# Attention of layer 2: the high and low parts of the values in one stationary operand, their products summed at the eviction

## The chip, the cores and the metric

The kernel runs on one core of a Trainium2 chip. The metric is device time in microseconds (us) of one execution. A core has five engines with a queue each, which work through it in order and meet at semaphores: PE (TensorE, matrix products), DVE (VectorE), ACT (ScalarE), POOL (GpSimd) and SP (SyncE, which here only issues DMAs). PE writes its products to PSUM, and ACT and DVE carry them from there to SBUF. Below, to evict means to read a result out of PSUM and write it to SBUF.

## The reference, cut to what matters

One inference step of two layers: a retention layer, then a layer of sliding-window attention, each for a prompt of 1024 tokens and for 8 decoding sequences of one token. The change is in the attention of the prompt in the second layer. There are 16 query heads of 64 elements and two key/value heads; eight query heads share one key/value head. A block of 128 queries sees its own block of keys and the one before it:

```python
scores = einsum('bnqkgd,bnskd->bnkgqs', qb, kk) * 64 ** -0.5      # 128 queries x 256 keys
scores = scores - alibi_slopes * dist                             # outside the band: -1e30
p = sink_softmax(scores, sinks)
o = einsum('bnkgqs,bnskd->bnqkgd', p, vv)                         # the product that is changed
y = x + (o * silu(gate)) @ w_out
```

Everything is computed to float32 accuracy. PE's fast format keeps fewer bits, so the kernel splits an operand x into a high part h (x rounded to the fast format) and a low part l = x - h, and forms a product of two such operands as h·h + h·l + l·h. That makes three passes through PE for each product.

## The kernel before, in words

Layer 1 and its output projection take the first two thirds of the time. Layer 2 begins with the keys and values: `kv_mm` projects them for eight chunks of 128 tokens, and `kv_ev` (lines 1269 to 1281) splits the values of a chunk into `vvh` (ACT, line 1272) and `vvl` (DVE, line 1273).

Then the heads are taken in pairs, eight pairs in all, and each pair in eight chunks of 128 queries, c = 0 to 7; a pair and a chunk make a unit, so there are 64 units. A generator (`pair_proj`) projects q and the gate of the next pair in steps of one slice of the weights, and the loop at the end of the program weaves three parts of three different units between these steps. In iteration m it does:

- `att_s` of unit m+4: four matmuls for the scores of both heads (lines 1477 and 1478), the scores scaled and biased to the tile `s` by DVE (line 1480, one instruction for each head), the negated row maximum by DVE (`mx`, line 1482), the exponentials with their sums by ACT (line 1484, two), the reciprocal of the sums by DVE (line 1485), and the division by POOL (line 1486);
- `att_x` of unit m+1: four transposes on PE (line 103 out to `tr`), their high part `pth` by ACT (line 1500) and low part `ptl` by DVE (line 1501);
- `att_o` of unit m: the products with the values. For each of the two key blocks (one block where c is 0) PE does three matmuls into the PSUM tile `o` of 64 partitions and 256 columns, which are 128 queries of each of the two heads: `vvh`·`pth`, `vvl`·`pth`, `vvh`·`ptl` (lines 1516 to 1518). ACT evicts the two heads to the two halves of `ot` (line 1521, two instructions of 64 partitions by 128 columns, scaled by 0.5), and POOL multiplies with the gate (line 1522). The last chunk of each token group writes `ot` to DRAM, issued by ACT (line 1527).

Between these parts `fill` puts steps of the projection for about 0.95 us each. `o` has one PSUM bank, so the matmuls of a unit wait until the tile of the unit before it is evicted; `sc` and `tr` have two. The evictions of the projection stand on ACT (lines 1365 to 1367, 1410) and DVE (lines 1368, 1370, 1408, 1411). From unit 50 on the low parts of the last weights are made by DVE (line 1061) instead of POOL, and from unit 59 on the steps woven in are those of the output projection. Reloads of earlier pairs from DRAM (`reload3`, lines 1617 to 1619) and the attention of the decoding sequences (from line 1540) fall there too.

The order of PE's instructions is that of the program text (`manual_schedule` over PE alone). The order on ACT, DVE, POOL and SP is chosen by a scheduler when the program is built, and is fixed from then on: an instruction that waits holds up all that stand behind it on its engine.

## Time and profile before

| | |
|---|---|
| median of 3 runs | 1365.5 us (1363.65 to 1366.26) |
| the profiled execution | 1365.26 us, of which the span of instructions is 1363.5 us |
| PE busy | 1309.2 us, 96% of the span |
| weight loads (PEld) busy | 1247.8 us, 92% |
| DVE busy | 742.0 us, 54% |
| ACT busy | 670.0 us, 49% |
| POOL busy | 760.6 us, 56% |
| granted PE clock, mean | 0.991 of full speed |
| attention of layer 2 | from about 985 to 1276 us of the span |

The busy time of an engine is the union of its instructions. A row of the table of groups names the line of the program, the engine, the operation, out<-in, the shape, the number of instructions, then the busy time of all and the mean time of one; behind the bar stands the time the engine sat idle just before such instructions, and what ended it. A row "A <- B" of the table of waits says that instructions A began when B was done, with the total time, how often, and the longest. Matmuls are pipelined: one lasts longer in the records than the distance from its start to the start of the next, and this distance is what a matmul costs in a dense stretch. DVE and ACT overlap neighbours a little as well.

### The profile page before, as it was taken

What the parts mean: (1) busy time and instruction counts of PE and PEld (TensorE: products, weight loads), DVE (VectorE), ACT (ScalarE), POOL (GpSimd) and SP (SyncE); (2) the same over time, 40 slices, a digit from 0 to 9 for tenths busy, and PEclk for the clock granted to TensorE, in tenths of its full rate; (3) what the DMA queues carried; (4) which work ended last, traced back from release to release, by engine and by line L of the source; (5) the groups of instructions that cost most, each with busy time, mean ns of one, the idle gap of its engine ahead of it and who ended that gap; (6) DMA issues with size and microseconds to landing.
All of it is one profiled execution on the core that took longest, in us unless ns stands there. A gap on an engine that the chain in (4) does not pass through costs nothing.

```text
span 1363.5 us, 25993 instructions
## 1 busy us (share of the span) xinstructions
PE 1309.2 (96%) x9541; PEld 1247.8 (92%) x9541; DVE 742.0 (54%) x1434; ACT 670.0 (49%) x1690; POOL 760.6 (56%) x886
## 2 busy tenths in 40 slices
PE   6999999999999999897979999998999999999998
PEld 6999999999999999686867889997999999998998
DVE  6943665666566553675762112325567777779421
ACT  5532545555556653575750111244476666667311
POOL 6753656656565763597986464563366666544000
PEclk9999999999999999899999999999999999999999
DMA  6314767677676752565645444461111110112532
GB/s 219 103 55 145 218 208 230 173 225 232 188 232 187 233 166 84 184 175 186 171 154 170 124 147 126 132 187 48 51 47 47 44 47 32 49 33 90 173 83 82
DMA packets 192803, 186.66 MB, mean 137 GB/s; under 512 B 12724, under 2 KB 172524, under 8 KB 192660
## 3 DMA queue, kind: packets, MB, share of 16 engines
q1 hardware_dynamic: 155776, 147.82, 36.1%
q10 hardware_dynamic: 36900, 37.19, 8.6%
q8 instruction: 75, 1.23, 0.4%
q14 instruction: 52, 0.43, 0.1%
HBM read 128.59 MB, written 57.41 MB: 136 GB/s over the span
## 4 chain that ended last, share of the span: by engine, by line
PE 81%; DVE 6%; POOL 4%; DMA 4%; ACT 2%; issue 2%; SPq 0%; ACTq 0%; POOLq 0%; DVEq 0%
PE b L340 7%; PE b L342 7%; PE b L341 7%; PE pj L1071 5%; PE pj L1072 5%; PE pj L1073 5%; PE b L334 4%; PE b L333 4%; PE b L335 4%; PE pj L1122 4%; PE pj L1120 4%; PE pj L1121 4%; PE tr L103 3%; POOL wl L1061 1%; PE tr L862 1%
## 5 line engine op out<-in xcount | busy, mean ns | idle before, releaser
L340 PE MATMUL b<-xh,woh 128*128 128x258 f32 x784 | 222.2, 283 | 0.0
L342 PE MATMUL b<-xh,wol 128*128 128x258 f32 x784 | 221.7, 283 | 0.0
L341 PE MATMUL b<-xl,woh 128*128 128x258 f32 x784 | 221.4, 282 | 0.0
L1071 PE MATMUL pj<-A_hi,wh 128*128 128x384 f32 (+1 forms) x512 | 171.7, 335 | 1.9 <-ACT Qd L1375 1.9
L1072 PE MATMUL pj<-A_lo,wh 128*128 128x384 f32 (+1 forms) x512 | 164.8, 322 | 0.0
L1073 PE MATMUL pj<-A_hi,wl 128*128 128x384 f32 (+1 forms) x512 | 164.7, 322 | 0.0
L1061 POOL TENSOR_TENSOR wl<-wr,wh 128x512 fp32r<-128x512 f32 (+1 forms) x68 | 125.4, 1857 | 53.3 <-DVE wh L1060 22.3
L340 PEld LDWEIGHTS b<-xh,woh 128*128 128x128 f32 x784 | 148.1, 189 | 1.1
L341 PEld LDWEIGHTS b<-xl,woh 128*128 128x128 f32 x784 | 148.7, 190 | 0.0
L342 PEld LDWEIGHTS b<-xh,wol 128*128 128x128 f32 x784 | 148.0, 189 | 0.0
L334 PE MATMUL b<-wol,xh 128*128 128x256 f32 x448 | 126.0, 281 | 1.2 <-DVE wol L224 1.2
L333 PE MATMUL b<-woh,xh 128*128 128x256 f32 x448 | 125.8, 281 | 0.0
L335 PE MATMUL b<-woh,xl 128*128 128x256 f32 x448 | 125.7, 281 | 0.0
L1486 POOL TENSOR_TENSOR s<-s,sm 128x512 f32<-128x512 f32 x64 | 67.7, 1059 | 75.4 <-DVE sm L1485 71.5
L282 POOL TENSOR_TENSOR yl<-yd,yh 128x256 fp32r<-128x256 f32 x64 | 56.4, 882 | 83.8 <-PE od L289 39.0
L1071 PEld LDWEIGHTS pj<-A_hi,wh 128*128 128x128 f32 x512 | 97.0, 189 | 2.4 <-ACT Qd L1375 2.2
L1072 PEld LDWEIGHTS pj<-A_lo,wh 128*128 128x128 f32 x512 | 97.0, 189 | 0.0
L1073 PEld LDWEIGHTS pj<-A_hi,wl 128*128 128x128 f32 x512 | 96.8, 189 | 0.0
L224 POOL TENSOR_TENSOR wol<-raw,woh 128x512 fp32r<-128x512 f32 x52 | 68.8, 1330 | 48.1 <-ACT woh L219 48.0
L334 PEld LDWEIGHTS b<-wol,xh 128*128 128x128 f32 x448 | 84.3, 188 | 1.4 <-DVE wol L224 1.4
L333 PEld LDWEIGHTS b<-woh,xh 128*128 128x128 f32 x448 | 84.3, 188 | 0.7
L335 PEld LDWEIGHTS b<-woh,xl 128*128 128x128 f32 x448 | 84.4, 188 | 0.0
(366 smaller groups left out, 3826.3 us busy)
## 6 DMA issues: line engine op xcount, KB each, us to landing
raw<-in_w_in_ret_dram ACTq DMA_DIRECT2D x44, 512.0 KB
st<-in_state_ret_dram SPq DMA_DIRECT2D x64, 256.0 KB
out_dram<-st SPq DMA_DIRECT2D x64, 256.0 KB
wr<-in_w_out_ret_dram SPq DMA_DIRECT2D x32, 512.0 KB
wr<-in_w_in_swa_dram SPq DMA_DIRECT2D x18, 512.0 KB
vb<-vscr SPq DMA_DIRECT2D x64, 128.0 KB
evp<-qks SPq DMA_DIRECT2D x32, 256.0 KB
evx<-vsc SPq DMA_DIRECT2D x32, 256.0 KB
```

What stands on the lines that cost most here:

```text
L224: eng.tensor_tensor(lo, src_of(s, name, sub), hi.bitcast(F32), SUB)
L333: mm(dst, xh, wh, start=a and i == 0, stop=False, skip_group_check=True)
L334: mm(dst, xh, wl, start=False, stop=False, skip_group_check=True)
L335: mm(dst, xl, wh, start=False, stop=z, skip_group_check=True)
L340: mm(dst, wh, xh, start=a, stop=False, **sg)
L341: mm(dst, wh, xl, start=False, stop=False, **sg)
L342: mm(dst, wl, xh, start=False, stop=z, **sg)
L1061: lo_eng[0].tensor_tensor(lo[:, js, :], raw[:, i:i + step, :], hi.bitcast(F32)[:, js, :], ALU.subtract)
L1071: mm(ps, hi[:, k, fs], xh[:, k, t0:t1], start=first and k == ks[0], stop=False)
L1072: mm(ps, hi[:, k, fs], xl[:, k, t0:t1], start=False, stop=False)
L1073: mm(ps, lo[:, k, fs], xh[:, k, t0:t1], start=False, stop=last and k == ks[-1])
L1486: nc.gpsimd.tensor_tensor(st[:, :, 0:256], st[:, :, 0:256], sm.unsqueeze(2).broadcast_to([128, 2, 256]), ALU.mult)
```

## The change

The values of a chunk now lie in one tile `vv`, with the high and the low part of each key/value head side by side: 64 columns high, 64 columns low. One matmul with this operand of 128 columns gives `vvh`·`pth` in the partitions 0 to 63 of `o` and `vvl`·`pth` in the partitions 64 to 127. The pass with `ptl` goes to the partitions 0 to 63 as before. So `o` has 128 partitions, a key block needs two matmuls in place of three, and the two halves have to be added at the eviction. ACT copies the upper half of the two heads, scaled by 0.5, to SBUF (one head to a new tile `t0`, one to its place in `ot`), and DVE adds the lower half to each (`scalar_tensor_tensor`, 64 partitions by 128 columns, one operand in PSUM). The tile `t0` has one buffer.

```diff
-        nc.scalar.activation(vvh[:, c, :], ps[:, 128:256], AF.Copy, scale=r)
-        nc.vector.scalar_tensor_tensor(vvl[:, c, :], ps[:, 128:256], r, vvh.bitcast(F32)[:, c, :],
-                                       ALU.mult, ALU.subtract)
+        pv = ps[:, 128:256].rearrange("p (g d) -> p g d", g=2)
+        nc.scalar.activation(vv[:, c, :, 0, :], pv, AF.Copy, scale=r)
+        nc.vector.scalar_tensor_tensor(vv[:, c, :, 1, :], pv, r, vvf[:, c, :, 0, :], ALU.mult, ALU.subtract)
...
-        po = opp.tile([64, 256], F32, tag="o", name="o")
-        vs = slice(u.g * 64, u.g * 64 + 64)
-        for hf in hs:
-            kc = c - 1 + hf
+
+        po = opp.tile([128, 256], F32, tag="o", name="o")
+        def pv(hf, low, **kw):
+            vs = vv[:, c - 1 + hf, u.g]
             rs_ = slice(hf * 256, hf * 256 + 256)
-            mm(po, vvh[:, kc, vs], pth[:, rs_], start=(hf == hs[0]), stop=False)
-            mm(po, vvl[:, kc, vs], pth[:, rs_], start=False, stop=False)
-            mm(po, vvh[:, kc, vs], ptl[:, rs_], start=False, stop=(hf == 1))
+            if low:
+                mm(po[0:64], vs[:, 0, :], ptl[:, rs_], start=False, **kw)
+            else:
+                mm(po, vs.rearrange("p a d -> p (a d)"), pth[:, rs_], **kw)
+
+        if c > 0:
+            pv(0, False, start=True, stop=False)
+            pv(0, True, stop=False)
+            pv(1, True, stop=False)
+            pv(1, False, start=False, stop=True)
+        else:
+            pv(1, False, start=True, stop=True)
+            pv(1, True, stop=True, skip_group_check=True)
         cs = slice(i * 128, i * 128 + 128)
+        t0 = atp.tile([128, 128], F32, name="t0", bufs=1)
+        t = (t0[64:128], ot[64:128, cs])
         for j in range(2):
-            nc.scalar.activation(ot[j * 64:j * 64 + 64, cs], po[:, j * 128:j * 128 + 128], AF.Copy, scale=0.5)
+            nc.scalar.activation(t[j], po[0:64, j * 128:j * 128 + 128], AF.Copy, scale=0.5)
+        for j in range(2):
+            nc.vector.scalar_tensor_tensor(ot[j * 64:j * 64 + 64, cs], po[64:128, j * 128:j * 128 + 128], 0.5, t[j],
+                                           ALU.mult, ALU.add)
         nc.gpsimd.tensor_tensor(ot[:, cs], ot[:, cs], gt[:, cs], ALU.mult)
```

In the changed kernel the lines behind the first hunk are one higher, and those behind `att_o` 16 higher: the scores stand in line 1481, the maximum in 1483, the reciprocal in 1486, `ptl` in 1502, ACT's copies in 1534 and DVE's additions in 1536.

DVE, a unit without projection work behind its scores (chunk 5 of the third pair). Before, the scores of one unit (`s`, two heads), their maximum, the `ptl` of an earlier unit, the reciprocal of the sums (`sm`), and then the scores of the next unit:

```order
L1480 SCALAR_TENSOR_TENSOR s_13431<-sc_13430,rq_13105,ndp_12837 128x256
L1480 SCALAR_TENSOR_TENSOR s_13431<-sc_13430,rq_13105,ndp_13131 128x256
L1482 TENSOR_REDUCE mx_13432<-s_13431 128x2
L1501 TENSOR_TENSOR ptl_13458<-tr_13452,pth_13457 128x512
L1485 RECIPROCAL sm_13433<-sm_13433 128x2
L1480 SCALAR_TENSOR_TENSOR s_13492<-sc_13491,rq_13185,ndp_12837 128x256
```

The same place now:

```order
L1481 SCALAR_TENSOR_TENSOR s_13450<-sc_13449,rq_13117,ndp_12845 128x256
L1481 SCALAR_TENSOR_TENSOR s_13450<-sc_13449,rq_13117,ndp_13144 128x256
L1483 TENSOR_REDUCE mx_13451<-s_13450 128x2
L1502 TENSOR_TENSOR ptl_13477<-tr_13471,pth_13476 128x512
L1486 RECIPROCAL sm_13452<-sm_13452 128x2
L1536 SCALAR_TENSOR_TENSOR ot_13433<-o_13486,t0_13491 64x128
L1536 SCALAR_TENSOR_TENSOR ot_13433<-o_13486,ot_13433 64x128
L1481 SCALAR_TENSOR_TENSOR s_13512<-sc_13511,rq_13198,ndp_12845 128x256
```

The two additions stand between the reciprocal of one unit and the scores of the next.

DVE, the place where the output products of two units (chunks 6 and 7 of the second pair) follow each other closely on PE. Before, with `sq` and `gt` the gate of the projection:

```order
L1485 RECIPROCAL sm_13264<-sm_13264 128x2
L1408 TENSOR_TENSOR sq_13331<-pj_13254,rbc_11586 128x384
L1480 SCALAR_TENSOR_TENSOR s_13316<-sc_13315,rq_13105,ndp_12837 128x256
L1480 SCALAR_TENSOR_TENSOR s_13316<-sc_13315,rq_13105,ndp_13131 128x256
L1411 SCALAR_TENSOR_TENSOR gt_13333<-gt_13333,sq_13331 128x384
L1482 TENSOR_REDUCE mx_13317<-s_13316 128x2
L1501 TENSOR_TENSOR ptl_13340<-tr_13336,pth_13339 128x256
```

The same place now:

```order
L1486 RECIPROCAL sm_13279<-sm_13279 128x2
L1409 TENSOR_TENSOR sq_13347<-pj_13269,rbc_11585 128x384
L1536 SCALAR_TENSOR_TENSOR ot_13313<-o_13314,t0_13319 64x128
L1536 SCALAR_TENSOR_TENSOR ot_13313<-o_13314,ot_13313 64x128
L1481 SCALAR_TENSOR_TENSOR s_13332<-sc_13331,rq_13117,ndp_12845 128x256
L1481 SCALAR_TENSOR_TENSOR s_13332<-sc_13331,rq_13117,ndp_13144 128x256
L1412 SCALAR_TENSOR_TENSOR gt_13349<-gt_13349,sq_13347 128x384
L1483 TENSOR_REDUCE mx_13333<-s_13332 128x2
L1502 TENSOR_TENSOR ptl_13356<-tr_13352,pth_13355 128x256
L1536 SCALAR_TENSOR_TENSOR ot_13313<-o_13359,t0_13364 64x128
L1536 SCALAR_TENSOR_TENSOR ot_13313<-o_13359,ot_13313 64x128
```

The additions of chunk 6 stand behind `sq`, ahead of the scores; those of chunk 7 behind the `ptl` of that place.

PE, the products of chunk 6. Before:

```order
L1516 MATMUL o_13299<-pth_13234,vvh_11582 64x256
L1517 MATMUL o_13299<-pth_13234,vvl_11583 64x256
L1518 MATMUL o_13299<-ptl_13235,vvh_11582 64x256
L1516 MATMUL o_13299<-pth_13234,vvh_11582 64x256
L1517 MATMUL o_13299<-pth_13234,vvl_11583 64x256
L1518 MATMUL o_13299<-ptl_13235,vvh_11582 64x256
```

The same place now, with the first step of the projection behind it:

```order
L1520 MATMUL o_13314<-pth_13248,vv_11582 128x256
L1518 MATMUL o_13314<-ptl_13249,vv_11582 64x256 x2
L1520 MATMUL o_13314<-pth_13248,vv_11582 128x256
L1071 MATMUL pj_13269<-A_hi_7708,wh_12907 128x384
L1072 MATMUL pj_13269<-A_lo_7709,wh_12907 128x384
```

Six matmuls have become four; what stands before and behind them on PE is as it was.

More of the change, by code (lines that the diff above doesn't have):

```diff
@@ L1232, in _trunk @@
     kkl = kvp.tile([128, 2, NP], F32R, name="kkl")
-    vvh = kvp.tile([128, 8, 128], F32R, name="vvh")
-    vvl = kvp.tile([128, 8, 128], F32R, name="vvl")
+    vv = kvp.tile([128, 8, 2, 2, 64], F32R, name="vv")
+    vvf = vv.bitcast(F32)
     kdd = kvp.tile([8, 128], F32, name="kdd")
```

## The prediction

> **What bounds the kernel now.** I read the page first, then the busy time in windows, the waits of PE and DVE, the groups, the timeline of one pair, and the chain that ended last.

> ```profile
> span 1363.5 us, 25993 instructions
> PE 1309.2 (96%) x9541; PEld 1247.8 (92%) x9541; DVE 742.0 (54%) x1434; ACT 670.0 (49%) x1690; POOL 760.6 (56%) x886
> ```

> The averages make PE the bound and DVE half idle. The change lies in one stage only, so I took windows there (core 0: PE, PEld, DVE, ACT, POOL busy, then PE clock, DMA share, GB/s): the start of the attention, its even part, one pair of heads in it, and its end.

> ```profile
> 966.00:985.00 19.00, 17.14 (x104) 16.71 (x103) 11.10 (x23) 7.22 (x24) 5.29 (x7) 0.91 0.01 2
> 985.00:1222.00 237.00, 235.43 (x1714) 232.04 (x1713) 170.21 (x369) 160.82 (x476) 148.89 (x214) 1.00 0.13 41
> 1102.53:1139.34 36.81, 36.81 (x273) 36.42 (x271) 26.69 (x59) 22.95 (x71) 19.98 (x33) 1.00 0.09 29
> 1222.40:1262.40 40.00, 36.80 (x281) 35.11 (x281) 37.97 (x80) 29.33 (x83) 18.69 (x24) 1.00 0.29 90
> ```

> A pair takes 36.81 us, and PE is busy in all of it; the even part of 237 us is 237 / 36.81 = 6.44 such pairs. DVE is busy for 26.69 us of a pair, 73%. At the end, from 1222.4 to 1262.4, it is DVE that is full: 37.97 of 40 us. The chain that ended last says the same; in the even part it is matmuls, here it steps from DVE to DVE:

> ```profile
> 1255.02 0.59 DVE wl L1061
> 1255.61 1.15 DVE rbc L1564
> 1256.76 0.79 DVE s L1480 x2
> 1257.55 0.59 DVE ptl L1501
> 1258.14 1.13 DVE t L1568
> ```

> So there are two stages with two limits, and the change takes from PE and gives to DVE. What DVE waits for inside the pair (1102.53 to 1139.34), in total, times and longest:

> ```profile
> DVE s L1480 <- PE sc L1478: 4.0, 4, 1.9
> DVE sm L1485 <- ACT s L1484: 2.0, 5, 0.6
> DVE qs L1368 <- ACT qs L1367: 1.8, 3, 1.4
> DVE gt L1411 <- ACT gt L1410: 0.8, 2, 0.5
> DVE ptl L1501 <- ACT pth L1500: 0.6, 2, 0.3
> ```

> Of 10.12 idle us (36.81 - 26.69) only 4.0 are waits for the scores from PE. The others are waits for ACT, inside a queue that runs in order.

> **PE's part: 120 matmuls fewer.**

> ```profile
> L1516 PE MATMUL o<-pth,vvh 128*64 128x256 f32 x120 | 35.0, 292 | 3.1 <-ACT ot L1521 3.1
> L1517 PE MATMUL o<-pth,vvl 128*64 128x256 f32 x120 | 33.4, 278 | 0.0
> L1518 PE MATMUL o<-ptl,vvh 128*64 128x256 f32 x120 | 33.6, 280 | 0.3 <-DVE ptl L1501 0.2
> L1477 PE MATMUL sc<-kkh,qs 128*128 128x256 f32 x112 | 29.1, 282 | 0.0
> ```

> Their mean of 280 ns is not their cost, because they overlap. The cost is the distance between starts:

> ```profile
> 1123.41 0.28 PE L1516 MATMUL o<-pth,vvh 128*64 128x256 f32 x1
> 1123.53 0.28 PE L1517 MATMUL o<-pth,vvl 128*64 128x256 f32 x1
> 1123.65 0.28 PE L1518 MATMUL o<-ptl,vvh 128*64 128x256 f32 x1
> 1123.77 0.34 PE L1071 MATMUL pj<-A_hi,wh 128*128 128x384 f32 x1
> 1124.82 0.28 PE L1477 MATMUL sc<-kkh,qs 128*128 128x256 f32 x1
> 1124.93 0.28 PE L1478 MATMUL sc<-kkl,qs 128*128 128x256 f32 x1
> ```

> From 1123.41 to 1123.77 three take 0.36 us, about 0.117 us each. L1477 has a stationary operand of 128 columns and the next follows 0.11 us later, so the wider operand costs PE nothing. A unit loses two matmuls (one where c is 0), a pair 15, which is 15 x 0.117 = 1.76 us, and all 120 lose 14.0 us. A pair on PE alone would take 36.81 - 1.76 = 35.05 us. The `ptl` pass moves from third to second place and so needs `ptl` 0.12 us sooner; L1518 waited 0.2 us for it in all, so between nothing and 64 x 0.12 = 7.7 us, and I take nothing, since that one row shows one wait in 120.

> **The split of the values in `kv_ev`.** The same eight instructions on ACT and DVE with the same 128 elements for each partition, only in two pieces of 64. Nothing is added; I put it at zero, with a tenth of a microsecond either way for each.

> **ACT's part.** Two copies for a unit before and after. The nearest row is themselves, so they stay at 0.27 us each:

> ```profile
> L1521 ACT ACTIVATE ot<-o 64x128 f32<-64x128 f32 x128 | 34.0, 266 | 8.8 <-PE o L1518 7.5
> 1124.65 0.54 ACT L1521 ACTIVATE ot<-o 64x128 f32<-64x128 f32 x2
> ```

> **DVE's part: 128 additions more.** No row shows 64x128 with one operand in PSUM. The nearest is the same operation at 128 columns, the scores of a first chunk, alone and two in a row:

> ```profile
> L1480 DVE SCALAR_TENSOR_TENSOR s<-sc,rq,ndp 128x128 f32<-128x128 f32 x16 | 4.9, 346 | 3.1 <-PE sc L1478 2.6 <-POOL s L1486 0.4
> 1111.69 0.61 DVE L1480 SCALAR_TENSOR_TENSOR s<-sc,rq,ndp 128x128 f32<-128x128 f32 x2 [0.19 <-POOL s L1486]
> ```

> Two in a row take 0.61 us. The bounds are 0.54 (ACT's pair above) and 0.69 (2 x 346 ns); I take 0.61, the same shape on the same engine. All 64 units: 39.0 us of DVE work against 14.0 us of PE work saved. [...]

> **What this does to a pair.** DVE's work becomes 26.69 + 8 x 0.61 = 31.57 us. If nothing but work counted, 35.05 us on PE would still hold it. But the queue is in order. The idle that PE paces goes away: the 4.0 us for scores, and the 0.6 for `pth`, which ACT makes right behind PE's transposes. 5.5 us are left. A new wait comes: the additions need ACT's two copies (0.54 us), which stand behind the exponentials, while the reciprocal that also waits for the exponentials takes only 0.17. In half of the eight chunks the additions stand directly behind the reciprocal, as in the first place of the order shown: 4 x 0.35 = 1.4 us. Against that, the three waits for `qs` (1.8 us) do not come from DVE's chain, and a DVE that arrives 0.61 us later at each finds them done. So 31.57 + 5.5 + 1.4 - 1.8 = 36.7 us, nearly what PE takes today. With all waits kept and the new one in every chunk it is 31.57 + 5.5 + 8 x 0.35 = 39.9; the lower end is PE's 35.05.

> **The single bank of `o`.** It now comes free after DVE's addition, not after ACT's copy, and PE's next products wait for that. Mostly some 4 us lie between, but once in a pair it is close (chunks 6 and 7, the second place of the order):

> ```profile
> 1124.78 0.17 DVE L1485 RECIPROCAL sm<-sm 128x2 f32<-128x2 f32 x1 [0.57 <-ACT s L1484]
> 1125.02 0.56 DVE L1408 TENSOR_TENSOR sq<-pj,rbc 128x384 f32<-128x384 f32 x1
> 1125.43 0.36 PE L1516 MATMUL o<-pth,vvh 128*64 128x256 f32 x1
> ```

> ACT's copies ended at 1125.19, just ahead of the products at 1125.43. Now the additions come behind `sq`: 1125.58 + 0.61 = 1126.2, and PE would be ready at 1125.43 - 0.23 = 1125.2. PE stands 1.0 us there, with two steps of the projection queued behind. Half of that I count, since DVE works on meanwhile: 36.7 + 0.5 = 37.2 us for a pair. The even part: 6.44 x (37.2 - 36.81) = +2.5 us. It gains nothing; the 1.76 us are used up by DVE's queue.

> POOL's product with the gate waits for DVE instead of ACT, and behind it the DMAs of `ot` on ACT's queue, 21 of them. Each comes up to 0.7 us later, 15 us of ACT at most; ACT idles 76 us of those 237, and I count nothing.

> **The end of the attention.** From 1222.4 to 1262.4 nine units are evicted; 9 x 0.61 = 5.5 us more on an engine that has 2.0 us idle: between 3.5 and, with the new wait in each, 8.6 us. I take 5.0, near the plain work. PE's saving there (9 x 0.23) buys nothing, as PE already idles 3.2 us. After 1262.4 three units are left with DVE idle: the last release is 0.6 us later, PE has 0.7 less to do, zero together. SP's loads and the output projection keep their place.

> **Sum.** +2.5 + 5.0 = +7.5 us on the profiled execution's 1365.26: 1373 us. The median of the runs, 1365.5, differs from it by a tenth of what separates the lowest run from the highest.

> **The rivals.** (a) Faster: DVE's waits shrink until PE's 35.05 us hold. -1.76 x 6.44 = -11.3, the end +3.5: 1357 us. For it speaks that 31.57 us of work fit; it needs DVE's idle to fall from 10.1 to 3.5 us in a pair, and PE never to stand at chunk 7. Against it speak 5.5 us of waits for ACT. (b) No change: PE holds, but pays the 1.0 us at chunk 7: -0.76 x 6.44 = -4.9, the end +5.0: 1365 us. (c) More: the loop from scores over exponentials and copies to the additions and the next scores sets the pace, 39.9 us: +20, the end +5.5: 1391 us. The point between mine and this is whether `qs` and `sm` still wait behind the additions. (d) The clock. In 966 to 985 PE was busy 90% of the time and the granted clock was 0.91; in 1222 to 1262 it was 92% and 1.00. If the pair grows past 35.05 / 0.90 = 38.9 us and the clock goes to 0.91, 237 x 0.09 = 21 us come on top: 1394 us. [...] That the wide operand is slower on PE is excluded by L1477.

> **How the numbers follow.** My forecast (1368 to 1381) 0.40, (a) 0.18, (b) 0.16, (c) 0.22, (d) 0.04. What a measurement of this kernel can tell from no change is about 0.2%, 2.7 us. Faster 0.18, same 0.16, slower 0.40 + 0.22 + 0.04 = 0.66. The range leaves out half of (a), a third of (c) and (d): 1358 to 1390.

> **What would show it.** In the trace of the changed kernel: 240 products into `o` at 0.117 us between starts (right), additions of 0.61 us a pair (wrong if over 0.75), a pair of about 37 us with DVE busy 31 to 32 of it, DVE waiting for ACT's copies and no longer for PE's scores, PE waiting for `o` by DVE about once in a pair, and the end longer by 3 to 9 us. A pair of 35 us with PE full makes me wrong on the low side; a pair near 40 on the high side.

## The result, and the profile after

The changed kernel takes 1386.99 us (median; 1385.68 to 1388.43), the kernel before beside it 1365.16 us: a ratio of 1.0155, 95% interval 1.0134 to 1.0175. It is slower, as forecast, but by 21.8 us where 7.5 were forecast: 1387 us lies outside the forecast's own 1368 to 1381, near the upper end of the wide range of 1358 to 1390.

For the comparison I cut the attention of layer 2 at rows of PE, since DVE's position lags behind. One mark is the last matmul into `pm` of a pair (line 1388 before, 1389 after), the other the first matmul of the decoding sequences' output (line 1596 before, 1612 after). The busy time in three windows of the kernel before: from the second to the last of the eight `pm` marks (the even part; the first mark, at 965.3, lies ahead of the attention), from there to the decoding output (the end), and the rest (the tail); columns as in the prediction:

```profile
1000.25:1232.22 231.97, 230.40 (x1678) 227.11 (x1678) 169.75 (x364) 158.70 (x468) 143.83 (x207) 1.00 0.15 46
1232.22:1274.01 41.79, 37.87 (x281) 35.41 (x280) 35.19 (x74) 27.36 (x77) 17.44 (x22) 1.00 0.33 101
1274.01:1363.50 89.49, 85.71 (x576) 84.49 (x576) 17.83 (x35) 17.97 (x45) 0.45 (x1) 1.00 0.38 108
```

The same windows of the changed kernel:

```profile
999.86:1238.38 238.52, 223.38 (x1581) 218.09 (x1580) 198.15 (x463) 158.03 (x466) 141.16 (x209) 1.00 0.14 44
1238.38:1295.62 57.24, 41.01 (x262) 37.70 (x262) 45.95 (x98) 28.49 (x80) 16.71 (x23) 0.88 0.28 89
1295.62:1386.60 90.98, 87.25 (x576) 85.97 (x576) 16.59 (x33) 16.63 (x43) 0.39 (x1) 0.98 0.36 100
```

The even part is 6.6 us longer, the end 15.4, the tail 1.5; with a start that is 0.4 earlier this makes the 23.1 us between the two spans. In the even part PE does 97 matmuls less and is busy for 7.0 us less, but stands still for 15.1 us instead of 1.6. DVE has 28.4 us more to do. In the end PE stands still for 16.2 us instead of 3.9, and the granted clock is 0.88 instead of 1.00, so what it does takes 3.1 us more although it has 19 instructions less.

The groups that the change made, in the changed kernel:

```profile
L1520 PE MATMUL o<-pth,vv 128*128 128x256 f32 x120 | 36.8, 306 | 24.1 <-DVE ot L1536 20.8 <-ACT wh L1058 1.9 <-ACT qs L1367 1.2
L1518 PE MATMUL o<-ptl,vv 128*64 128x256 f32 x120 | 24.9, 284 | 0.0
L1536 DVE SCALAR_TENSOR_TENSOR ot<-o,ot 64x128 f32<-64x128 f32 x64 | 18.9, 295 | 1.1
L1536 DVE SCALAR_TENSOR_TENSOR ot<-o,t 64x128 f32<-64x128 f32 x64 | 18.8, 293 | 11.3 <-ACT ot L1534 10.2
```

The additions take 0.59 us a unit, forecast 0.61. The number that was not foreseen in its size stands in the first row: PE waits 20.8 us, in all, for DVE to release `o` (the prediction had 1.0 us in each of some 6.4 pairs); the kernel before waited 3.1 us for ACT there. PE's waits of the changed kernel, first in the even part (window 985 to 1238.38), with all that is listed:

```profile
PE o L1520 <- DVE ot L1536: 11.1, 7, 2.6
PE o L1520 <- ACT wh L1058: 1.9, 1, 1.9
PE o L1520 <- ACT qs L1367: 1.2, 1, 1.2
PE pm L1387 <- ACT sq L1366: 0.6, 1, 0.6
```

The two rows at `o` that name ACT are waits for DVE too: both products began 0.14 to 0.15 us after the end of the second addition of the unit before, as in the first row, and `pth` and `ptl` of their units had been done for 1.6 us and more. The waits in the end (1238.38 to 1295.62), the three longest:

```profile
PE o L1520 <- DVE ot L1536: 9.6, 3, 4.9
PE sc L1478 <- DVE rbc L1571: 3.2, 1, 3.2
PE sc L1570 <- DVE s L1481: 1.7, 1, 1.7
```

The longest of them, in DVE's timeline of the changed kernel. PE's transposes before it began at 1248.08, and its next products at 1253.60:

```profile
1246.65 0.69 DVE L1061 TENSOR_TENSOR wl<-wr,wh 128x512 fp32r<-128x512 f32 x1
...
1247.45 0.43 DVE L1409 TENSOR_TENSOR sq<-pj,rbc 128x264 f32<-128x264 f32 x1
1247.80 2.01 DVE L1061 TENSOR_TENSOR wl<-wr,wh 128x512 fp32r<-128x512 f32 x2
1249.73 0.42 DVE L1412 SCALAR_TENSOR_TENSOR gt<-gt,sq 128x264 f32<-128x264 f32 x1
1250.08 0.68 DVE L1061 TENSOR_TENSOR wl<-wr,wh 128x512 fp32r<-128x512 f32 x1
...
1250.75 0.86 DVE L1481 SCALAR_TENSOR_TENSOR s<-sc,rq,ndp 128x256 f32<-128x256 f32 x2
1251.54 0.68 DVE L1502 TENSOR_TENSOR ptl<-tr,pth 128x512 fp32r<-128x512 f32 x1
1252.13 0.67 DVE L1483 TENSOR_REDUCE mx<-s 128x2 f32<-128x514 f32 x1
1252.84 0.29 DVE L1536 SCALAR_TENSOR_TENSOR ot<-o,t 64x128 f32<-64x128 f32 x1
1253.16 0.29 DVE L1536 SCALAR_TENSOR_TENSOR ot<-o,ot 64x128 f32<-64x128 f32 x1
```

ACT's copies for these additions were done at 1249.45. From then on DVE still had the rest of one low part of the last weights, the gate, another low part, the scores of a later unit, `ptl` and the maximum to do, and only then the two additions of 0.29 us. PE stood for 4.92 us. The single bank is not all of it: the `ptl` in this list belongs to the very products that wait, so with a free bank they would have stopped at their second matmul until 1252.21 (with two banks, below, PE waits 3.3 us for `ptl` there). The bank alone accounts for the last 1.4 us. At PE's other long stall in the end, from 1274.28 to 1278.43, `ptl` was done at 1275.43, and 3.0 of 4.14 us are the bank's.

### The profile page after: what moved, and what is told of

Read it like the earlier page. It is cut to its first block, busy times and chain, and to the rows that moved or that the text cites. A ratio compares the mean times of both kernels' runs of the same rounds, so it can differ in the third digit from the quotient of the medians.

```text
span 1386.6 us, 25980 instructions
## 1 busy us (share of the span) xinstructions
PE 1309.6 (94%) x9421; PEld 1245.5 (90%) x9421; DVE 780.5 (56%) x1562; ACT 669.5 (48%) x1690; POOL 756.8 (55%) x886
## 4 chain that ended last, share of the span: by engine, by line
PE 74%; DVE 10%; ACT 5%; issue 4%; POOL 3%; DMA 3%; ACTq 0%; SPq 0%; DVEq 0%; POOLq 0%
PE b L340 7%; PE b L342 7%; PE b L341 7%; PE pj L1122 4%; PE pj L1120 4%; PE pj L1121 4%; PE b L334 4%; PE b L333 4%; PE b L335 4%; PE pj L1071 3%; PE pj L1072 3%; PE pj L1073 3%; PE tr L103 3%; ACT s L1485 2%; DVE s L1481 2%
## 5 line engine op out<-in xcount | busy, mean ns | idle before, releaser
L1071 PE MATMUL pj<-A_hi,wh 128*128 128x384 f32 (+1 forms) x512 | 173.0, 338 | 2.0 <-ACT Qd L1376 1.9
L1061 POOL TENSOR_TENSOR wl<-wr,wh 128x512 fp32r<-128x512 f32 (+1 forms) x68 | 125.0, 1848 | 53.1 <-DVE wh L1060 16.7
L1071 PEld LDWEIGHTS pj<-A_hi,wh 128*128 128x128 f32 x512 | 97.8, 191 | 2.8 <-ACT Qd L1376 2.2
```

Source lines behind the costliest of these rows:

```text
L1061: lo_eng[0].tensor_tensor(lo[:, js, :], raw[:, i:i + step, :], hi.bitcast(F32)[:, js, :], ALU.subtract)
L1071: mm(ps, hi[:, k, fs], xh[:, k, t0:t1], start=first and k == ks[0], stop=False)
```

## The experiments

All of them in one table: time, ratio to the kernel before on the same chip, and the three parts as cut above. The parts are those of the one profiled execution and begin between 997 and 1002 us; the times are medians.

| kernel | us | ratio (95%) | even | end | tail | clock in the end |
|---|---|---|---|---|---|---|
| before | 1365.2 | 1 | 232.0 | 41.8 | 89.5 | 1.00 |
| changed | 1387.0 | 1.0155 (1.0134 to 1.0175) | 238.5 | 57.2 | 91.0 | 0.88 |
| products alone | 1364.7 | 0.9999 (0.9990 to 1.0009) | 226.0 | 46.9 | 91.0 | 0.96 |
| additions alone | 1394.9 | 1.0214 (1.0196 to 1.0231) | 242.3 | 58.2 | 92.6 | 0.82 |
| first six pairs only | 1373.7 | 1.0062 (1.0047 to 1.0078) | 238.4 | 42.2 | 90.5 | 1.00 |
| last two pairs only | 1381.3 | 1.0125 (1.0104 to 1.0146) | 231.7 | 57.0 | 91.0 | 0.88 |
| one addition of two | 1383.7 | 1.0143 (1.0125 to 1.0160) | 233.2 | 56.8 | 92.6 | 0.85 |
| additions, bank free | 1395.9 | 1.0231 (1.0210 to 1.0251) | 250.5 | 52.6 | 89.5 | 0.94 |
| changed, two banks | 1386.3 | 1.0150 (1.0122 to 1.0178) | 241.9 | 52.4 | 89.5 | 0.87 |
| before, two banks | 1364.0 | 0.9983 (0.9974 to 0.9993) | 230.9 | 41.3 | 91.1 | 0.96 |
| changed, `wl` on POOL | 1382.3 | 1.0117 (1.0099 to 1.0134) | 238.6 | 52.5 | 89.5 | 0.93 |
| before, `wl` on POOL | 1373.0 | 1.0048 (1.0030 to 1.0066) | 231.7 | 48.6 | 92.6 | 0.93 |
| changed, r early | 1386.4 | 1.0150 (1.0135 to 1.0165) | 238.6 | 55.7 | 89.4 | 0.85 |
| products alone, r early | 1362.1 | 0.9982 (0.9968 to 0.9996) | 226.1 | 45.2 | 89.5 | 0.96 |
| before, r late | 1370.7 | 1.0039 (1.0026 to 1.0052) | 232.3 | 46.2 | 91.0 | 0.96 |
| changed, two banks and r early | 1383.8 | 1.0125 (1.0101 to 1.0149) | 246.0 | 50.8 | 89.4 | 0.87 |
| mix | 1365.0 | 1.0007 (0.9996 to 1.0017) | 231.4 | 42.7 | 89.4 | 0.96 |
| mix, two banks | 1359.9 | 0.9956 (0.9943 to 0.9969) | 227.6 | 41.8 | 89.5 | 0.96 |

**The two halves of the change.** The products alone (merged products, ACT copies the upper half as before, no additions):

```diff
-            nc.scalar.activation(t[j], po[0:64, j * 128:j * 128 + 128], AF.Copy, scale=0.5)
-        for j in range(2):
-            nc.vector.scalar_tensor_tensor(ot[...], po[64:128, j * 128:j * 128 + 128], 0.5, t[j], ALU.mult, ALU.add)
+            nc.scalar.activation(ot[j * 64:j * 64 + 64, cs], po[0:64, j * 128:j * 128 + 128], AF.Copy, scale=0.5)
```

> The merged matmuls alone: 240 products into o as in the change, but only the upper half is evicted, by ACT as before, and nothing is added; the product of the low values is left out of the result, so this is a time of the PE part alone. Theory A (the change loses on DVE's in-order queue): PE is freed of 14 us and DVE gets nothing, so the even part of the attention follows PE, 35.05 us for a pair, 6.44 x 1.76 = 11 us less, and the end, where DVE is full, gains nothing: 1352 to 1357 us. Theory C (the wide operand or the new order of the passes costs PE time): 1365 us or more.

The additions alone (the three products of before, and two additions of zero times `o` that hold the bank):

```diff
-            nc.scalar.activation(ot[j * 64:j * 64 + 64, cs], po[:, j * 128:j * 128 + 128], AF.Copy, scale=0.5)
+            nc.scalar.activation(t[j], po[:, j * 128:j * 128 + 128], AF.Copy, scale=0.5)
+        for j in range(2):
+            nc.vector.scalar_tensor_tensor(ot[...], po[:, j * 128:j * 128 + 128], 0.0, t[j], ALU.mult, ALU.add)
```

> The additions alone: the three matmuls of before, but ACT copies the two heads to a new tile and to ot, and DVE then writes ot from both with the same instruction as in the change (64 x 128, the operand in PSUM multiplied by zero). The bank of o is held until DVE is done. Theory A: DVE's queue and the held bank are the loss, so the time is that of the change or a little above, since PE has its 14 us still: 1385 to 1396 us. Theory C: the additions are nearly free, 1365 to 1369 us.

The additions alone came out inside their expectation, 29.8 us slower. The products alone missed theirs: 1364.7 us, no gain at all. The even part did gain, 6.0 us of the 97 x 0.117 = 11.3 us that the spacing of dense matmuls promises; then the end gave back 5.1 and the tail 1.5. So PE's saving was worth little before any addition came. Beside the additions it was worth more, 1394.9 - 1387.0 = 7.9 us.

**Where the loss lies.** The merged form in the first six pairs only, then in the last two only (`MIXP` is 6, the other pairs have the products of before):

```diff
+        if u.p < MIXP:        # first six; for the last two: u.p >= MIXP
             po = opp.tile([128, 256], F32, tag="o", name="o")
...
+        else:
+            po = opp.tile([64, 256], F32, tag="o", name="o")
...
```

> The change in the first six of the eight pairs; the last two pairs, whose output products fall in the end of the attention where DVE is full, have three matmuls and ACT's eviction as before. Theory A: the even part costs what it does in the traces, +4 to +7 us, and the end's +15 us go away: 1368 to 1373 us. If what the change does in the even part is what makes the end long (work arriving late), the time stays above 1378 us.

> The merged form only in the last two pairs of heads, the form of before in the first six; the complement of the kernel with the first six alone, which cost 8.5 us of the 21.8. If the loss of the end is its own (additions of the last units queue behind the last weights' low parts, TensorE stands still and its clock falls), the two add up: 1376 to 1382 us. If the end loses only because VectorE comes to it late from the first six pairs: 1366 to 1371 us.

The two make 8.7 and 17.2 us, together even more than the 21.8 of the whole change. Six pairs lengthen the even part by 6.4 us and hardly touch the end; the last two pairs, a quarter of the units, lengthen the end by 15.2 us. PE's stall of 4.92 us at `o` is in that kernel too. The first missed its range by 0.7 us, the second lies inside. So the end's loss is made by its own 16 units and not by DVE arriving late.

**How it grows.** The changed kernel with only the first of its two additions:

```diff
-        for j in range(2):
+        for j in range(1):
             nc.vector.scalar_tensor_tensor(ot[j * 64:j * 64 + 64, cs], po[64:128, j * 128:j * 128 + 128], 0.5, t[j],
```

> The changed kernel with one of its two additions a unit: the low product of the second head of each pair is left out of the output. With no additions the time was 1364.7 us, with both 1387. Theory A, in the form that VectorE is full everywhere: the loss grows in proportion, 1374 to 1378 us. Theory A with a threshold (the first 0.3 us a unit still finds waits to lie in, the stalls and the slower clock come with the second): 1366 to 1371 us.

Neither expectation held. In the even part the loss does grow with DVE's work: 226.0 us without additions, 233.2 with one, 238.5 with two. In the end it is a step: 46.9, 56.8, 57.2. The first addition of 0.29 us does nearly all the harm there, so the end's loss does not follow the time of the additions; what came with the first of them are waits for it, the late chain of r (below) and a lower clock (0.85). PE's three longest waits in the end of this kernel (1234.87 to 1291.67):

```profile
PE o L1520 <- DVE ot L1536: 3.8, 2, 2.0
PE o L1520 <- ACT s L1485: 3.6, 1, 3.6
PE sc L1478 <- DVE rbc L1571: 3.4, 1, 3.4
```

The 3.6 us are again DVE's: the product began 0.14 us after the addition of the unit before it.

**The single bank.** First the additions with the old products, but reading ACT's copies in SBUF, so that the bank comes free after ACT (they add zero times the copy to itself):

```diff
+            nc.scalar.activation(t0[j * 64:j * 64 + 64, :], po[:, j * 128:j * 128 + 128], AF.Copy, scale=0.5)
+        for j in range(2):
+            js = slice(j * 64, j * 64 + 64)
+            nc.vector.scalar_tensor_tensor(ot[js, cs], t0[js, :], 0.0, t0[js, :], ALU.mult, ALU.add)
```

> As the additions alone, but ACT copies both heads to a tile in SBUF and DVE reads that tile only, so the bank of o is free after ACT as before; DVE has as many instructions as in the change and POOL waits for them. Theory A1 (DVE's time and order are the loss, the bank matters little): the even part as in the change, the end some 5 to 15 us longer, 1380 to 1390 us. Theory A2 (half of the loss or more is PE waiting for the one bank behind additions that stand far back in DVE's queue): 1368 to 1377 us.

Then a second bank for `o`, in the changed kernel and, as a control, in the kernel before. The bank comes from `ms`, whose tiles move to `tr` and `pj`:

```diff
-    msp = ctx.enter_context(tc.tile_pool(name="msp", bufs=1, space=PSUM))
-    opp = ctx.enter_context(tc.tile_pool(name="opp", bufs=1, space=PSUM))
+    opp = ctx.enter_context(tc.tile_pool(name="opp", bufs=2, space=PSUM))
...
-            pm = msp.tile([128, 512], F32, tag="ms", name="pm")
+            pm = trp.tile([128, 512], F32, name="tr")
```

> The changed kernel with two PSUM banks for o in place of one. The bank comes from the pool of the squares' sums, which now use the banks of the transposes, and the output projection holds two open accumulators in place of three. Theory B (PE waiting for the one bank, 20.8 us in the trace of the change, is the loss): 1366 to 1376 us. Theory A (DVE's time and its order; a second bank only lets PE run ahead of a DVE that is late): 1380 to 1388 us.

> The same banks in the kernel before, as the control: PE waits there for o 3.1 us in all, so 1363 to 1368 us; above that, the other banks that were changed cost something by themselves, and the run with two banks is to be read against this one.

The additions with the bank free, at 1395.9 us, lie above both their expectations. The changed kernel with two banks lies in the range of theory A, its control in its own. In the whole time the bank seems to be nothing: 1386.3 against 1387.0 us. By parts it is something: the end falls from 57.2 to 52.4 us with two banks, and from 58.2 (additions alone) to 52.6 with the bank freed by ACT. The 4.8 us of the second bank are about what the two stalls above leave to it, 1.4 and 3.0 us; waits for `ptl` stay, 5.3 us in the end. But the even part takes the gain back. PE's longest wait there in the changed kernel with two banks (1000 to 1240.72), and what ACT did before one of the longest of these:

```profile
PE tr L1386 <- ACT sq L1365: 11.0, 12, 1.7
```

```profile
1035.34 0.33 ACTq L1542 DMA_DIRECT2D oscr<-ot  x1
1035.71 0.49 ACT L1365 ACTIVATE sq<-pj 128x384 f32<-128x384 f32 x1 [2.43 <-POOL ot L1537]
```

The squares `sq`, which PE needs next, stand on ACT behind the DMA of `ot`. That waits for POOL's product with the gate (1034.85 to 1035.31), for which DVE's additions were done at 1033.91 only. At this place of the changed kernel with one bank the squares stand ahead of the DMA (1034.79 and 1036.07), so the order on ACT has moved too. Sharing the banks of `tr` costs nothing by itself: the kernel before with two banks has an even part of 230.9 us for 232.0. So this run does not show what the bank is worth in the even part. The test with the bank free is no clean one for the even part either: its additions, with both operands in SBUF, took 440 ns in the mean instead of 294.

**What stands ahead of the additions.** The low parts of the last weights back on POOL, in the changed kernel and in the kernel before:

```diff
-            lo_eng[0] = nc.vector
+            pass
```

> The changed kernel, but the low parts of the last weights stay on POOL to the end (16 instructions of 0.6 to 0.7 us taken from DVE, about 11 us, all in the end of the attention). If DVE's time at the end is what costs (theory A), the end shrinks from 54 to 44 to 48 us: 1376 to 1381 us. If it is the single bank and the place of the additions alone (theory B), or POOL becomes the late one, 1384 us or more.

> The same move of the low parts of the last weights to POOL in the kernel before, as the control: DVE is full there too, but PE idles 3 to 4 us only, so between 1361 and 1368 us by either theory.

Both missed on the slow side, by 1.3 us above the nearer range and by 5.0: on POOL the low parts stand ahead of the product with the gate, ACT once waits 5.6 us for that product with its DMA of `ot`, and the kernel before loses 6.4 us by the move. Against this control the change costs 9.3 us in all and 3.9 us in the end, instead of 21.8 and 15.4. So the end's loss seems to need a DVE that is full with other work; but the control has a stall of its own, 7.0 us of PE at `o` behind ACT, which may cover a part.

**The order on DVE.** One more thing moved in the built program. The decoding sequences need r, the reciprocal root for their scores (lines 1542 to 1546 before). In the kernel before the scheduler puts this chain far ahead of its use; DVE's timeline there:

```profile
1236.75 0.13 DVE L1542 TENSOR_TENSOR r<-ms,rbc 16x8 f32<-16x8 f32 x1
...
1242.14 0.13 DVE L1546 TENSOR_TENSOR r<-r,rbc 16x8 f32<-16x8 f32 x1
1248.21 0.67 DVE L1555 TENSOR_TENSOR rbc<-sc,r 16x512 f32<-16x512 f32 x1
```

In the changed kernel, and in every kernel whose last pairs have the merged form or additions, it stands three units later, just ahead of its use (only with `wl` on POOL does it start sooner):

```profile
1259.05 0.13 DVE L1558 TENSOR_TENSOR r<-ms,rbc 16x8 f32<-16x8 f32 x1
...
1263.07 0.99 DVE L1562 TENSOR_TENSOR r<-r,rbc 16x8 f32<-16x8 f32 x1 [1.45 <-POOL r L118]
1264.16 1.28 DVE L1571 TENSOR_TENSOR rbc<-sc,r 16x512 f32<-16x512 f32 x2
```

Here DVE waits for POOL, the scores wait for DVE, and PE for the scores' tiles (3.2 us). Three kernels move this chain alone: in the changed kernel and in the products alone it is written four units earlier, and in the kernel before it is held back by an instruction that reads the maximum of unit 61 and adds zero.

```diff
         if m == 56:
             drain(ps)
+            dec_r()           # the lines of r, taken out of dec_scores
             so_ahead(2)
```

```diff
         nc.vector.tensor_tensor(r16, ms16, rr, ALU.mult)
+        nc.vector.scalar_tensor_tensor(r16, mxl[0][0:16, 0:1].broadcast_to([16, 8]), 0.0, r16, ALU.mult, ALU.add)
```

> The changed kernel with the chain r of the decoding sequences (four small DVE instructions and POOL's reciprocal root) taken out of the decoding scores and written four units earlier, where the kernel before has it in DVE's order; the changed kernel has it three units later, just ahead of the scores that need it. Theory O (order: part of the end's loss is that the scheduler moved this chain, so that DVE waits for POOL and PE for DVE): the wait of PE for rbc (3.2 us) and DVE's for r (1.45 us) go, 1381 to 1384 us. Theory A (only the additions' time and their place behind the low parts of the weights): 1386 to 1388 us.

> The merged products alone, without the additions (the lower half of o is left out of the output), and the same chain r four units earlier. With r late this kernel took 1364.7 us: it gained 7.3 us in the even part and lost 4.7 in the end, where PE waited 3.0 us for rbc. Theory O: the end is as before and the gain stays, 1356 to 1361 us. If the end loses for another reason: 1363 to 1366 us.

> The kernel before with the chain r held back until the maximum of unit 61 is there, by one small instruction that adds nothing to r but reads that maximum; DVE's order of the chain is then that of the changed kernel. No additions, old products. Theory O: 1367 to 1371 us, the end 3 to 5 us longer, with PE waiting for rbc. If r has room enough: 1364 to 1366 us.

With r late the kernel before loses 5.4 us with no addition in it, its end is 4.4 us longer, and PE waits as in the changed kernel (window 1229 to 1276):

```profile
PE sc L1477 <- DVE rbc L1560: 3.1, 1, 3.1
PE sc L1559 <- DVE r L1547: 1.0, 1, 1.0
```

So the place of four small instructions is worth 5 us there. The products alone gain 2.6 us by the early chain (the two intervals overlap a little) and miss the expectation by 1 us, as their end stays 3.4 us longer than before. The kernel before with r late lies inside the expectation of theory O. The changed kernel gains 0.6 us, which is nothing: PE's wait for `rbc` is gone, and the one for `o` has grown (PE's first row in the window 1215 to 1310 of the changed kernel with r early; 12.5 of it lie in the end, where the changed kernel has 9.6):

```profile
PE o L1520 <- DVE ot L1536: 13.7, 4, 6.9
```

The early chain now stands in front of that unit's additions, with DVE's wait of 1.53 us for POOL in it. The last run took both away, the one bank and the late chain:

> The changed kernel with two banks for o and the chain r of the decoding sequences four units earlier, both at once. From the last milestone (row rq of the last pair) to the decoding products the kernel before took 39.3 us, the changed one 54.2, with two banks 47.6; the kernel before with the chain late took 43.8. Theory S (the end's 15 us are a sum: some 6.5 for the one bank, 4.5 for the late chain, 4 to 5 for the additions' own time): the end falls to 43 to 44 us, the whole to 1381 to 1384 us. Theory T (the waits replace each other, as the early chain alone gave only 1.6 us): the end stays at 46 to 48 us, the whole at 1385 to 1387.

Its two figures point to different theories: the total of 1383.8 us lies in the range of the sum, the end does not. The marks of that expectation lie on DVE; from the last of them the end takes 46.1 us, as the theory of replaced waits had it, and from PE's mark 50.8. The wait for `rbc` is gone again, and one for `ptl`, also DVE's, has grown from 3.3 to 5.3 us. (Its profiled execution was the slowest of its four, with an even part of 246.0 us, so that part isn't read.) Here a full DVE passed its lateness to whoever waited next.

**A version that beats both.** DVE had room where the kernel before let it wait for the scores, above all in chunks 1, 2 and 4 of a pair. The merged form there only, first in six pairs, then in pairs 1 to 5 with two banks:

```diff
+        if u.c in (1, 2, 4) and 1 <= u.p < 6:   # the first mix: u.p < 6
```

> The merged form (two wide products, two additions) only in chunks 1, 2 and 4 of the first six pairs of heads; every other chunk and the last two pairs have the three products of the kernel before. Theory A (VectorE, which works its queue in order, has room only where the kernel before let it wait for the scores, 23.1 us in 26 waits, most of them in the first chunks of a pair; an addition costs time only where that room is used up): the additions fall into the waits, TensorE keeps 6 x 2 x 3 units at 0.117 x 2 = 8 us at most, and the end of the kernel is untouched: 1359 to 1364 us. Theory C (any unit with additions costs, whatever its place, since TensorE's saving comes to nothing at the end even alone): 1367 to 1371 us, 3/8 of what all units of the six pairs cost (8.5 us) and more.

> A candidate to beat both: two banks for o (the kernel before gained 0.2% with them) and the merged form only in chunks 1, 2 and 4 of pairs 1 to 5, without the first pair, which lost 3.2 us where all chunks 1, 2, 4 of six pairs had it. If the gains add: 1357 to 1361 us. If the additions again only use up what PE saves: 1362 to 1365 us.

The first mix, at 1365.0 us, fell between its two expectations; the first stretch between two marks, which holds the end of the first pair and the start of the second, took 42.6 us against 40.5 before, with PE waiting 2.1 us for `o`, and used up what the others gained. In the second 15 units lose two matmuls each, 15 x 2 x 0.117 = 3.5 us, and against the kernel before with two banks the even part is 3.3 us shorter: here the whole saving arrives. DVE's waits for the scores show where the additions went; first the kernel before (1000 to 1232), then this one (998 to 1226), then all that PE waits in this one:

```profile
DVE s L1480 <- PE sc L1478: 19.5, 23, 1.9
```

```profile
DVE s L1481 <- PE sc L1479: 5.2, 14, 1.5
```

```profile
PE o L1546 <- DVE ptl L1502: 0.4, 1, 0.4
```

At 1359.93 us, ratio 0.9956 (0.9943 to 0.9969), it is faster than the kernel before, by 5.4 us, lies inside its expectation, and is, as far as the intervals tell, faster than the kernel before with two banks (0.9974 to 0.9993).

## Why the prediction was wrong in size

- **The sign held, and in the even part the reason.** PE's saving is used up by waits for DVE's queue, and the time goes up. The prices of the single instructions held as well: 0.59 us of additions a unit for 0.61, wide matmuls at the spacing of the narrow ones (in the median 0.119 us from the start of a wide one to the next start, 0.116 to 0.118 from a narrow one before).
- **The pair was nearly right.** Forecast were 37.2 us, a DVE busy for 31.6 and no waits for PE's scores. A pair of the changed kernel, its busy times and DVE's waits:

```profile
1105.10:1141.98 36.88, 34.97 (x249) 34.14 (x249) 30.49 (x74) 23.06 (x71) 18.82 (x31) 1.00 0.09 30
```

```profile
DVE sm L1486 <- ACT s L1485: 1.7, 3, 0.6
DVE ot L1536 <- ACT ot L1534: 1.3, 3, 0.7
DVE qs L1369 <- ACT qs L1368: 0.9, 2, 0.5
DVE gt L1412 <- ACT gt L1411: 0.9, 2, 0.7
DVE ptl L1502 <- ACT pth L1501: 0.3, 1, 0.3
```

  Here the pair is cut at DVE's scores. Between PE's marks the quiet pairs take 37.5 and 37.6 us, and in the second (1117.38 to 1154.96) PE is busy for 35.73 us and stands for 1.85. So the saving of 1.76 us a pair was put too high: PE's busy time fell from 36.80 to 35.73, and in the products alone the same pair takes 35.5 us, 1.3 less than before.
- **The even part was put too low, +2.5 for +6.6, in the term for the single bank.** It said 1.0 us at chunk 7 and counted half, "since DVE works on meanwhile". PE stood 1.6 to 1.7 us at that place in five pairs (1.68 in the one above), and all of it counts: PE was free at 1128.39, ACT's copies, which the prediction had done by then, at 1129.08, the second addition at 1129.93, and the products began at 1130.07. And the even part was taken as 6.44 equal pairs: the first stretch has two stalls of its own behind DVE's additions, 1.9 and 2.6 us, and the pairs in which weights are loaded lose 1.0 and 1.4 us instead of the 0.6 and 0.8 of the quiet ones.
- **The end was the step that failed, +5.0 for +15.4, and 1.5 more in the tail.** It counted the additions as work on a full engine, nine units by 0.61 us. The runs show a step that one addition sets off as well as two. Three things were not in the sum: waits of PE for this queue, for the bank (some 5 us of the end, 57.2 against 52.4 with two) and for `ptl`; the order of DVE's other work, which was taken over from the kernel before although the scheduler makes it anew (4.4 us by the late chain, in a kernel with nothing else changed); and a slower clock (0.88: PE is busy 3.1 us longer with 19 instructions less). These don't simply add up, since taking one away let the next wait grow (with r early PE's wait for `o` in the end was 12.5 us, not 9.6).
- **A slower clock at the end was not foreseen.** The single-bank stall was worked out for a quiet pair only, at 1.0 us. At the end, where the same wait stands behind the weights' low parts and the decoding sequences' softmax, it came to 4.92 and 4.14 us, and the granted clock was 0.50 from 1251.19 to 1258.02, the first 2.4 us of it while PE still stood, and from 1278.50 to 1281.91, right behind the other stall. Rival (d) itself, a slower clock in the even part, did not come true. Its mark for the clock, a share of busy PE below 90% over a whole stage, was not met in the even part (94%, clock 1.00); in the end the clock fell at single stalls, as the windows in the last section show for the kernel with r early too.
- **"After 1262.4 zero"** was wrong too: the tail pays 1.5 us, all at its beginning, where the clock falls once more (0.51 from 1298.90 to 1302.40, 1.00 before and after).
- **"Each comes up to 0.7 us later ... I count nothing"**, of the DMAs of `ot` on ACT, did no visible harm in the changed kernel, but in the one with two banks PE's waits behind such a DMA used up most of what the bank gained.
- **The rivals.** (c) was nearest in time, for a wrong reason: no loop of 39.9 us paces the pairs. (a) and (b) needed PE's saving to reach the end, and even without additions it did not (1364.7 us).

What stays open: why the scheduler moves the chain r; why the products alone get only 6.0 of 11.3 us in the even part, of which PE's standing still explains 2.2 (from the matmul ahead of a unit's products to the one behind them, a unit became 0.22 us shorter where a step of the projection stands ahead, but 0.14 behind transposes and 0.18 behind `pm`); and how much of the end's loss is the clock's, since no run holds it at 1.00 with the stalls in place.

## What to carry to other kernels

When the release of a PSUM bank moves from one engine to another, look up what stands ahead of it in that engine's queue at each stage, not what the new instruction costs: one addition of 0.3 us a unit cost 10 us in the end, where the queue was full, with the waits and the lower clock that came with it, and 7 us over the six pairs where it had room. Then look at what else the same consumer needs from that queue (here `ptl`): a second bank takes away only what the bank adds to that, here 4.8 of the 15.4 us in the end. Where a scheduler sets the order, compare the order of all the other work in the built program too; a small chain that slipped just ahead of its use cost 5.4 us by itself. Apply such an exchange only in the places where the engine that gets the work is seen waiting for the one that is relieved; here that paid with two banks and without the first pair, and with one bank in six pairs it gained nothing.

## What the runs showed of the hardware that was not expected

- **The clock fell after a single stall, and stayed low after it.** In the changed kernel with r early PE stood from 1249.40 to 1256.25. Five windows there, cut where the granted clock changes or at the same length:

```profile
1251.08:1254.50 3.42, 0.00 (x0) 0.00 (x0) 3.06 (x8) 0.00 (x0) 0.47 (x2) 1.00 0.18 53
1254.50:1257.91 3.41, 1.66 (x8) 1.69 (x8) 3.32 (x9) 1.09 (x4) 1.20 (x2) 0.50 0.84 255
1257.91:1261.32 3.41, 2.81 (x13) 1.57 (x13) 2.34 (x7) 2.68 (x8) 1.02 (x3) 0.50 0.01 2
1261.32:1264.74 3.42, 3.42 (x31) 3.06 (x29) 2.90 (x7) 1.64 (x5) 1.34 (x2) 0.50 0.03 5
1264.74:1268.15 3.41, 3.39 (x23) 3.06 (x22) 3.28 (x7) 1.38 (x5) 1.60 (x2) 1.00 0.00 0
```

```profile
1174.96 1.09 POOL L1486 TENSOR_TENSOR s<-s,sm 128x512 f32<-128x512 f32 x1 [2.44 <-DVE sm L1485]
1175.19 1.02 DVE L1525 SCALAR_TENSOR_TENSOR ot<-t 64x128 f32<-64x128 f32 x1
```

  All 29 that began while the division had more than 0.2 us left ended 0.14 to 0.15 us after it, and took 356 to 1155 ns; the two of 1380 and 1382 ns ended so behind a low part `wl` on POOL. In the changed kernel, with one operand in PSUM, 44 additions began in the same way beside the division, and each took 292 to 296 ns.
